# Pairing the value products of successive attention steps and pinning TensorE's order in both mixers of a two-layer encoder trunk

## Chip, cores and metric

The kernel runs on one core of one Trainium2 chip, as one launch. The metric is device time in microseconds, the median of several runs of the same program. TensorE is named PE in the profile, VectorE DVE, ScalarE ACT, GpSimd POOL, and SP is the queue that issues the DMAs.

## The reference

The trunk has two layers on a sequence of 1024 tokens with 1024 features, all in float32, and a final RMSNorm. Layer 0 mixes with two head groups side by side, layer 1 with a chunked band; each mixer is followed by a SwiGLU of width 2816.

```python
# layer 0: MLA (8 heads) | stick-breaking (8 heads), one input projection, one output projection
s_a = (q_a @ k_a.T) * scale_a                       # q_a, k_a from normed latents, with rotary parts
p_a = softmax(where(chunk_ok, s_a, -inf)); o_a = p_a @ v_a
z = (q_b @ k_b.T) * scale_b
log_keep = where(before, log_sigmoid(-z), 0)
w_b = where(before, exp(log_sigmoid(z) + (reverse_cumsum(log_keep) - log_keep)), 0); o_b = w_b @ v_b
h = h + concat(o_a, o_b) @ w_out
# layer 1: every chunk of 64 sees itself and the 8 chunks before it, 16 heads, bias by clipped distance
p = softmax(where(valid, q @ k.T * scale + bias, -inf)); o = p @ v
h = h + o @ w_out
# after each mixer
h = h + (silu(u @ w_gate) * (u @ w_up)) @ w_down    # u = rms_norm(h, g)
```

## The kernel before

Activations stand transposed, features over the 128 partitions, tokens in two halves of 512 columns. A float32 product is done in three matmuls of a shorter float format: each operand is split into a high and a low part (`split`, `weight`, L244 to L269), and `mm3` (L271) multiplies high by high, high by low and low by high. The FFNs use a scheme of seven block products; their order is written out by hand and pinned on all four compute engines.

In the mixers, heads go in pairs: four pairs of stick-breaking, four of MLA, eight of the band. A pair's attention runs over rows (a half of 512 queries) and, in a row, over steps (a block of 128 keys): 4 steps for the first half, 8 for the second. Steps whose block lies on the diagonal work on 512, 384, 256 or 128 columns. A step has stages: in stick-breaking `scores` (L879), `weights` (L897) and `outputs` (L920); in MLA and in the band `front` (scores, exponential, running sum of exponentials) and `back`, which are in `soft_step` (L1044). The last stage is the value product `weighted` (L815): for each of the two heads one matmul of 64 output columns, which the chip does in two passes. So a step shows as four 64-column matmuls on L819 in the profile. After the last step of an MLA or band row, `soft_finish` (L1072) sums the exponentials with ones (64-column matmuls on L1076) and divides.

`step` (L752) keeps a list of steps that still have stages to come. Each call first runs the next stage of every pending step, oldest first, then the first stage of the new step; empty stages set the delay. With `LAG = 2` the delays before the change are: stick-breaking, weights two calls after scores and outputs two calls after weights; MLA, `back` four calls after `front`; band, two calls.

`weave` (L773) interleaves an attention generator with a fill generator (the projections and values of the next pair, or an output projection): after each step it draws fill until the fill's cost is in proportion to the attention done. `with_max` (L1197) draws, after each step from number `skip` on, one group of row maxima (`mla_max`, `band_max`) for a row to come; groups left over when the row ends follow at once. A maximum's end is `neg_max_rows` (L1014): a reduction on VectorE (L1018), transposes of 4 output columns on TensorE (L1021), and VectorE writes (L1023) into the query operand that the scores of that row read. In the band the maxima of a group are passes of VectorE over scores in PSUM (L1166).

PSUM has three kinds of buffers, two of each: `mm` for projections, `o` for value products and norm sums, and `z`, of two banks, for scores, maxima, transposes and denominators. Weights are loaded by the SP queue into four raw buffers and split into four high and four low buffers.

`rstd` (L303) makes a norm's factor: a matmul with ones (L307), then a chain of ScalarE and VectorE operations. `columns` (L333) turns the factor into columns with eight one-column matmuls (L337). `close` (L327) calls both.

Outside the FFNs the order of instructions on each engine is not the source's: a scheduler sorts them by priority and by when it reckons their inputs to be ready. `keep_in_program_order` ties an instruction behind the one traced before it on its engine, as an order of issue alone; `Pinned` wraps an engine so that all its instructions get this.

Of the kernel before, what the change touches and what calls it, by code (L numbers as in the profile page):

```python
# [19 lines left out]
KD = D // P  # L20
# [10 lines left out]
LAG = 2  # L31
# [45 lines left out]
class PinnedCore:  # L77
    def __init__(self, tc):
        nc = tc.nc
        self.sync = nc.sync  # L80
        self.tensor, self.vector, self.scalar, self.gpsimd = (
            Pinned(tc, e) for e in (nc.tensor, nc.vector, nc.scalar, nc.gpsimd))
# [68 lines left out]
class Trunk:  # L151
# [711 lines left out]
    def sb_step(self, p, hf, j, proj, vt, st, o_d):  # L863
        nc = self.nc
# [5 lines left out]
        top = j == 4 * hf + 3  # L870
        c0 = r * P if diag else 0
        cs = slice(c0, HALF)
# [57 lines left out]
        idle = [lambda: None] * (LAG - 1)  # L930
        self.step(scores, *idle, weights, *idle, outputs)
# [112 lines left out]
    def soft_step(self, lag, scores, cs, st, vt, j, first, last, dest):  # L1044
# [25 lines left out]
        self.step(front, *[lambda: None] * (lag - 1), back)  # L1070
# [19 lines left out]
    def mla_attend(self, p, hf, proj, vt, o_d):  # L1090
# [5 lines left out]
        for j in range(nj):  # L1096
# [16 lines left out]
            self.soft_step(2 * LAG, scores, cs, st, vt, j, j == 0, j == nj - 1, (o_d[hf], p, p == 3))  # L1113
# [59 lines left out]
    def band_attend(self, p, hf, proj, tk, vt, o_d):  # L1173
# [5 lines left out]
        for n, j in enumerate(order):  # L1179
# [14 lines left out]
            self.soft_step(LAG, scores, cs, st, vt, j, n == 0, n == len(order) - 1, (o_d[hf], p, p == 7))  # L1194
# [26 lines left out]
    def mixer0(self, h_d):  # L1221
# [5 lines left out]
        with self.phase("mix0", MIX0_TEMPS):  # L1227
# [21 lines left out]
            for p in range(4):  # L1249
                nxt = ([[], []], [[], []], [])  # L1250
                if p < 2:
                    vw = [a["w_vb"][2], a["w_vb"][3]]
                    fill, cost = self.chain(self.sb_project(p + 1, u, nxt), vgen(vw, 1, [p])), 31.0
                elif p == 2:
                    fill, cost = self.chain(self.sb_project(3, u, nxt), self.rope_key(u)), 31.0
                else:
                    fill, cost = prepare(), 73.0
                self.weave(self.ending(self.sb_attend(p, proj, vts[p], o_d)) if p == 3 else
                           self.sb_attend(p, proj, vts[p], o_d), 9.24, fill, cost)
                proj = nxt  # L1260
            for p in range(4):
                nxt = ([[], []], [[], []])
                first, second = (self.mla_attend(p, hf, mla, va[p], o_d) for hf in range(2))
                top = lambda hf: self.mla_max(hf, mla)
                if p < 3:
                    att = self.chain(self.with_max(first, top(1), 0), self.with_max(second, self.mla_max(0, nxt), 4))
                    fill, cost = self.mla_project(p + 1, cq, ckv, nxt), 13.0
                    if p == 2:
                        fill, cost = self.mla_project(3, cq, ckv, nxt, "c", [0]), 8.0
                    self.weave(att, 7.0, fill, cost)  # L1270
                else:
                    o_p = [[None] * KD, [None] * KD]
                    first = self.with_max(first, self.out_loads(o_d[0], 3, o_p[0]), 0)
                    second = self.with_max(second, self.out_loads(o_d[1], 3, o_p[1]), 0)
                    fill = self.chain(self.mla_project(3, cq, ckv, mla, "c", [1]), self.free(top(1)))
                    self.weave(self.ending(first), 2.5, fill, 4.0)
                    o_p[0][3] = o_d[0][3]
                    self.weave(self.ending(second), 6.5, half(0), 41.5)
                    o_p[1][3] = o_d[1][3]
                mla = nxt  # L1280
        return out, half(1, 1)

    def mixer1(self, u, h_d, h2_d):
        a = self.a
        o_d = self.spill("o1_")
        out = Stream()
        half = lambda hf, *e: self.out_half(hf, a["w_out1"], o_p[hf], lambda hf, m: h_d[hf][m], list(range(KD)), out,
                                            h2_d, *e)
        with self.phase("band", BAND_TEMPS):
            vts = [[] for _ in range(8)]  # L1290
            vgen = lambda g, hf: self.values([a["w_v1"][2 * g], a["w_v1"][2 * g + 1]], u, 4, KD, 1,
                                             vts[2 * g:2 * g + 2], hf)
            self.now(vgen(0, [0, 1]))
            new = lambda: ([[], []], [[], []])
            proj = new()
            self.now(self.band_project(0, u, proj))
            tq, tk = self.band_bias(0, "bias_q"), self.band_bias(0, "bias_k")
            self.now(self.band_max(0, proj, tq))
            for p in range(8):
                nxt, fill, cost, tqn, tkn = new(), iter(()), 0.0, None, None  # L1300
                if p < 6:
                    fill = self.chain(self.band_project(p + 1, u, nxt), vgen(p // 2 + 1, [p % 2]))
                    cost = 28.0
                elif p == 6:
                    fill, cost = self.band_project(7, u, nxt, [0]), 16.0

                def late(p=p, nxt=nxt):
                    nonlocal tqn, tkn
                    tqn, tkn = self.band_bias(p + 1, "bias_q"), self.band_bias(p + 1, "bias_k")
                    yield from self.band_max(0, nxt, tqn)  # L1310

                first, second = (self.band_attend(p, hf, proj, tk, vts[p], o_d) for hf in range(2))
                top = self.band_max(1, proj, tq)
                if p < 7:
                    self.weave(self.chain(self.with_max(first, top, 1), self.with_max(second, late(), 4)), 6.8,
                               fill, cost)
                else:
                    o_p = [[None] * KD, [None] * KD]
                    first = self.with_max(first, self.out_loads(o_d[0], 7, o_p[0]), 0)
                    second = self.with_max(second, self.out_loads(o_d[1], 7, o_p[1]), 0)  # L1320
                    fill = self.chain(self.band_project(7, u, proj, [1]), self.free(top))
                    self.weave(self.ending(first), 2.5, fill, 8.0)
                    o_p[0][7] = o_d[0][7]
                    self.weave(self.ending(second), 5.0, half(0), 41.5)
                    o_p[1][7] = o_d[1][7]
                proj, tq, tk = nxt, tqn, tkn
        return out, half(1, 1)

    def run(self):
# [6 lines left out]
        def to_mixer1(hf, m):  # L1336
# [3 lines left out]
            if m == KD - 1:  # L1340
                self.close(nxt, hf, columns=True)
# [135 lines left out]
```

## Time and profile before

| | us |
|---|---|
| three runs | 2614.07, 2611.87, 2613.88 |
| median | 2613.88 |
| the profiled execution, its own time | 2617.44 |
| span of its trace, first to last instruction | 2615.4 |
| mean granted TensorE clock | 0.988 |

In the span the stages lie so: the start of layer 0 up to about 85 us, stick-breaking to 428, MLA to about 600, its output projection and FFN 0 to 1300, the band mixer to about 1900, FFN 1 to the end. An execution's own time is some 2 us above the span. A row of the timeline has the start, the duration, engine, line, operation, tile written and tiles read, shapes (contraction rows * output columns, then partitions x columns) and the count of neighbours merged into it; in square brackets stands the engine's idle time before it and what ended that. A row by groups has busy time and the mean of one in ns behind the bar. A row by windows has the stretch, its length, the busy time of each engine in the order PE, PEld (weight load), DVE, ACT, POOL (engines with nothing are left out), the granted clock and the DMA share.

### The profile page before, as it was taken

Reading aid. Unit: us, or ns where it says so; the run is one execution under the profiler, and the core shown is the slowest. Engines: PE = TensorE matmul, PEld = TensorE weight load, DVE = VectorE, ACT = ScalarE, POOL = GpSimd, SP = SyncE. Lnnn points to the kernel's source line nnn. Section 1 sums busy time; section 2 is a strip of 40 time slices with the busy share of each in tenths; the row PEclk is TensorE's granted clock in tenths of the full one; section 3 lists DMA queues with packets and bytes.
Section 4 is the critical chain, followed back from the end, with each engine's and each line's share of the span. In section 5 each row is a group of like instructions: output and inputs, shape, how many; then the busy total and the mean of one; then the engine's idle time right before and its main releaser. Section 6 shows DMA issues by size and latency. Waiting matters only on the chain.

```text
span 2615.4 us, 33607 instructions
## 1 busy us (share of the span) xinstructions
PE 2523.4 (96%) x11758; PEld 1945.9 (74%) x11758; DVE 1911.0 (73%) x3072; ACT 1169.3 (45%) x2028; POOL 520.4 (20%) x489
## 2 busy tenths in 40 slices
PE   7999999999989999999999999999999999999997
PEld 6766765557878888887887766676777888888776
DVE  6888887775886666677666777777688666667775
ACT  4776676454444434433253333334444443443224
POOL 3333324663000000000022333335300000000004
PEclk9999999999999999999999999999999999999999
DMA  4221100125434334476642222222543434447561
GB/s 137 61 63 53 53 17 29 35 69 160 150 121 141 112 134 145 150 261 215 206 152 67 73 82 80 70 69 89 173 161 119 142 109 137 142 151 258 204 213 69
DMA packets 178856, 318.65 MB, mean 122 GB/s; under 512 B 20480, under 2 KB 36736, under 8 KB 178688
## 3 DMA queue, kind: packets, MB, share of 16 engines
q1 hardware_dynamic: 178688, 316.51, 36.7%
q8 instruction: 93, 1.52, 0.2%
q14 instruction: 75, 0.61, 0.1%
HBM read 221.53 MB, written 84.41 MB: 117 GB/s over the span
## 4 chain that ended last, share of the span: by engine, by line
PE 70%; DVE 12%; issue 2%; ACT 1%; DMA 1%; SPq 0%; DVEq 0%; ACTq 0%
PE z L74 24%; PE mm L74 14%; PE o L74 6%; PE mm L274 5%; PE mm L275 5%; PE mm L276 5%; PE o L819 3%; DVE u L74 2%; DVE f L1081 2%; PE z L1189 1%; PE z L1163 1%; PE z L1190 1%; DVE u L297 1%; PE z L1076 1%; PE z L1108 1%
## 5 line engine op out<-in xcount | busy, mean ns | idle before, releaser
L74 PE MATMUL z<-u,wh 128*128 128x512 f32 x992 | 312.6, 396 | 20.9 <-DVE u L74 13.0
L74 PE MATMUL z<-u,vh 128*128 128x512 f32 x992 | 308.0, 392 | 0.0
L274 PE MATMUL mm<-u,wh 128*128 128x512 f32 x720 | 291.6, 405 | 2.5 <-DVE u L699 1.2
L275 PE MATMUL mm<-u,wh 128*128 128x512 f32 x720 | 284.6, 395 | 1.4 <-DVE u L242 1.4
L276 PE MATMUL mm<-u,wl 128*128 128x512 f32 x720 | 283.8, 394 | 0.0
L242 POOL TENSOR_TENSOR wl<-wr,wh 128x512 fp32r<-128x512 f32 (+2 forms) x95 | 122.7, 1298 | 803.9 <-ACT wh L237 735.3
L74 PEld LDWEIGHTS z<-u,wh 128*128 128x128 f32 x992 | 188.4, 191 | 65.2 <-ACT wh L74 18.0
L74 PE MATMUL mm<-u,wh 128*128 128x512 f32 x720 | 222.5, 390 | 0.0
L74 PEld LDWEIGHTS z<-u,vh 128*128 128x128 f32 x992 | 187.6, 189 | 40.3 <-issue 1.0
L74 PE MATMUL z<-u,wl 128*128 128x512 f32 x496 | 195.5, 394 | 0.0
L74 PE MATMUL z<-u,vl 128*128 128x512 f32 x496 | 193.4, 390 | 0.0
L274 PEld LDWEIGHTS mm<-u,wh 128*128 128x128 f32 x720 | 135.6, 188 | 62.5 <-issue 33.3
L819 PE MATMUL o<-a,u 128*64 128x512 f32 (+3 forms) x768 | 172.3, 485 | 0.3 <-ACT a L1192 0.3
L275 PEld LDWEIGHTS mm<-u,wh 128*128 128x128 f32 x720 | 135.8, 189 | 32.6 <-issue 8.3
L276 PEld LDWEIGHTS mm<-u,wl 128*128 128x128 f32 x720 | 135.6, 188 | 32.2 <-issue 3.7
L74 PEld LDWEIGHTS mm<-u,wh 128*128 128x128 f32 x720 | 135.2, 188 | 28.9 <-issue 1.0
L74 PE MATMUL mm<-u,vh 128*128 128x512 f32 x496 | 152.7, 389 | 0.0
L242 POOL TENSOR_TENSOR u<-wr,u 128x512 fp32r<-128x512 f32 x8 | 10.9, 1373 | 673.6 <-ACT u L237 673.6
L74 PE MATMUL mm<-u,wl 128*128 128x512 f32 x360 | 140.1, 389 | 0.0
L1192 ACT ACTIVATE a<-a 128x1024 f32<-128x1024 f32 (+3 forms) x96 | 70.6, 738 | 155.4 <-DVE a L1191 155.1
L1060 POOL TENSOR_TENSOR b<-b,a 128x512 f32<-128x512 f32 (+3 forms) x80 | 110.5, 1381 | 135.9 <-ACT a L1192 120.4
L1191 DVE TENSOR_TENSOR a<-z,bias 128x1024 f32<-128x1024 f32 (+3 forms) x96 | 78.7, 823 | 79.5 <-PE z L1190 65.5
(246 smaller groups left out, 5972.3 us busy)
## 6 DMA issues: line engine op xcount, KB each, us to landing
u<-f_t SPq DMA_DIRECT2D x144, 256.0 KB, 5.2
vr<-in_w_up SPq DMA_DIRECT2D x88, 256.0 KB, 4.0
wr<-in_w_gate SPq DMA_DIRECT2D x88, 256.0 KB, 3.5
f_t<-x SPq DMA_DIRECT2D x72, 256.0 KB, 2.0
wr<-in_w_out SPq DMA_DIRECT2D x64, 256.0 KB, 3.0
f_t<-e SPq DMA_DIRECT2D x54, 256.0 KB, 3.5
ld<-f SPq DMA_DIRECT2D x54, 256.0 KB, 5.2
h<-u SPq DMA_DIRECT2D x48, 256.0 KB, 2.3
```

The costliest lines, as they stand in the source:

```text
L74: return lambda *a, **k: self.tc.keep_in_program_order(f(*a, **k))
L242: self.eng(eng).tensor_tensor(lo, src, hi.bitcast(F32), ALU.subtract)
L274: mm(out, wh, xh, start=first, stop=False, skip_group_check=onto)
L275: mm(out, wh, xl, start=False, stop=False, skip_group_check=onto)
L276: mm(out, wl, xh, start=False, stop=last, skip_group_check=onto)
L297: self.eng(eng).tensor_tensor(acc, acc, sq, ALU.add)
L819: self.nc.tensor.matmul(o[rh, cs], vt[j // 4][:, j % 4, rh], w[:, e, cs], start=first, stop=last)
L1060: self.eng("dve" if dest[2] else "pool").tensor_tensor(st["esum"][:, :, cs], old[:, :, cs], ex[:, :, cs], ALU.add)
L1076: nc.tensor.matmul(den[64 * e:64 * e + 64, :], self.ones[:, 0:64], esum[:, e, :], start=True, stop=True)
L1081: nc.vector.scalar_tensor_tensor(r, t, 2.0, r, ALU.add, ALU.mult)
L1191: nc.vector.tensor_tensor(ex[:, :, cs], z[:, :, cs], tk[:, :, xs], ALU.add)
L1192: nc.scalar.activation(ex[:, :, cs], ex[:, :, cs], AF.Exp)
```

## The change

`PinnedCore` takes the names of the engines to pin. The pairs' loops of both mixers now run with TensorE alone pinned; the other engines, and the SP queue, stay with the scheduler. The delays are set by the parity of the step, so that a step and its successor have their last stage in the same call: in stick-breaking the outputs come two calls after the weights for odd key blocks and one call after for even ones; in MLA `back` comes four calls after `front` for even steps and three for odd ones; in the band three and two. In the latent norms of MLA, `columns` becomes a piece of its own, drawn later. At the start of the band mixer, the values of the first pairs are formed half by half (each call loads and splits the weights), and the second half's `close`, before made at the end of FFN 0, stands between the first half's values and the first projection.

```diff
-    def __init__(self, tc):
...
+    def __init__(self, tc, names):
+        for n in ("sync", "tensor", "vector", "scalar", "gpsimd"):
+            e = getattr(tc.nc, n)
+            setattr(self, n, Pinned(tc, e) if n in names else e)
...
-    def pinned(self):
-        nc, self.nc = self.nc, PinnedCore(self.tc)
+    def pinned(self, names=("tensor", "vector", "scalar", "gpsimd")):
+        nc, self.nc = self.nc, PinnedCore(self.tc, names)
...
         idle = [lambda: None] * (LAG - 1)
-        self.step(scores, *idle, weights, *idle, outputs)
+        self.step(scores, *idle, weights, *idle[(j + 1) % 2:], outputs)
...
-            self.close(s, hf, (384, 256)[g], g == 1)
+            self.close(s, hf, (384, 256)[g])
             yield
+            if g:
+                self.columns(s, hf, self.out_bank())
+                yield
...
-    def soft_step(self, lag, scores, cs, st, vt, j, first, last, dest):
+    def soft_step(self, n, lag, scores, cs, st, vt, j, first, last, dest):
...
-        self.step(front, *[lambda: None] * (lag - 1), back)
+        self.step(front, *[lambda: None] * (lag - 1 - n % 2), back)
...
-            self.soft_step(2 * LAG, scores, cs, st, vt, j, j == 0, j == nj - 1, (o_d[hf], p, p == 3))
+            self.soft_step(j, 2 * LAG, scores, cs, st, vt, j, j == 0, j == nj - 1, (o_d[hf], p, p == 3))
...
-            self.soft_step(LAG, scores, cs, st, vt, j, n == 0, n == len(order) - 1, (o_d[hf], p, p == 7))
+            self.soft_step(n, LAG + 1, scores, cs, st, vt, j, n == 0, n == len(order) - 1, (o_d[hf], p, p == 7))
...
# mixer0: the loops over the pairs of stick-breaking and of MLA, unchanged, go under
+            with self.pinned(["tensor"]):
...
# mixer1: all of the mixer but its last output half goes under
+            with self.pinned(["tensor"]):
...
-            self.now(vgen(0, [0, 1]))
+                self.now(vgen(0, [0]))
+                self.close(u, 1, columns=True)
...
+                self.now(self.band_project(0, u, proj))
+                self.now(vgen(0, [1]))
...
# run, at the end of FFN 0
-            if m == KD - 1:
+            if m == KD - 1 and hf == 0:
                 self.close(nxt, hf, columns=True)
```

More of the change, by code (lines that the diff above doesn't have):

```diff
@@ L77 @@
 class PinnedCore:
-    def __init__(self, tc):
[L79 to L82, printed above, removed]
+    def __init__(self, tc, names):
+        for n in ("sync", "tensor", "vector", "scalar", "gpsimd"):
+            e = getattr(tc.nc, n)
+            setattr(self, n, Pinned(tc, e) if n in names else e)
 class Pair:
@@ L1247, in prepare @@
                 yield from self.free(self.mla_max(0, mla))
[L1249 to L1280, printed above, removed]
@@ L1289, in mixer1 @@
         with self.phase("band", BAND_TEMPS):
-            vts = [[] for _ in range(8)]
-            vgen = lambda g, hf: self.values([a["w_v1"][2 * g], a["w_v1"][2 * g + 1]], u, 4, KD, 1,
-                                             vts[2 * g:2 * g + 2], hf)
-            self.now(vgen(0, [0, 1]))
[L1294 to L1326, printed above, removed]
@@ new lines, in mixer1, with late @@
+            with self.pinned(["tensor"]):
+                vts = [[] for _ in range(8)]
+                vgen = lambda g, hf: self.values([a["w_v1"][2 * g], a["w_v1"][2 * g + 1]], u, 4, KD, 1,
+                                                 vts[2 * g:2 * g + 2], hf)
+                self.now(vgen(0, [0]))
+                self.close(u, 1, columns=True)
+                new = lambda: ([[], []], [[], []])
+                proj = new()
+                self.now(self.band_project(0, u, proj))
+                self.now(vgen(0, [1]))
+                tq, tk = self.band_bias(0, "bias_q"), self.band_bias(0, "bias_k")
+                self.now(self.band_max(0, proj, tq))
+                for p in range(8):
+                    nxt, fill, cost, tqn, tkn = new(), iter(()), 0.0, None, None
+                    if p < 6:
+                        fill = self.chain(self.band_project(p + 1, u, nxt), vgen(p // 2 + 1, [p % 2]))
+                        cost = 28.0
+                    elif p == 6:
+                        fill, cost = self.band_project(7, u, nxt, [0]), 16.0
+                    def late(p=p, nxt=nxt):
+                        nonlocal tqn, tkn
+                        tqn, tkn = self.band_bias(p + 1, "bias_q"), self.band_bias(p + 1, "bias_k")
+                        yield from self.band_max(0, nxt, tqn)
+                    first, second = (self.band_attend(p, hf, proj, tk, vts[p], o_d) for hf in range(2))
+                    top = self.band_max(1, proj, tq)
+                    if p < 7:
+                        self.weave(self.chain(self.with_max(first, top, 1), self.with_max(second, late(), 4)), 6.8,
+                                   fill, cost)
+                    else:
+                        o_p = [[None] * KD, [None] * KD]
+                        first = self.with_max(first, self.out_loads(o_d[0], 7, o_p[0]), 0)
+                        second = self.with_max(second, self.out_loads(o_d[1], 7, o_p[1]), 0)
+                        fill = self.chain(self.band_project(7, u, proj, [1]), self.free(top))
+                        self.weave(self.ending(first), 2.5, fill, 8.0)
+                        o_p[0][7] = o_d[0][7]
+                        self.weave(self.ending(second), 5.0, half(0), 41.5)
+                        o_p[1][7] = o_d[1][7]
+                    proj, tq, tk = nxt, tqn, tkn
```

32 lines of the change are left out of this document (added).

## The prediction

> **What bounds the kernel now.** I read the page first, then the busy times by stretch, then the order of instructions on TensorE.
>
> ```profile
> span 2615.4 us, 33607 instructions
> PE 2523.4 (96%) x11758; PEld 1945.9 (74%) x11758; DVE 1911.0 (73%) x3072; ACT 1169.3 (45%) x2028; POOL 520.4 (20%) x489
> PE 70%; DVE 12%; issue 2%; ACT 1%; DMA 1%; SPq 0%; DVEq 0%; ACTq 0%
> ```
>
> The chain that ended last runs over TensorE for 70% and over VectorE for 12%. Busy TensorE time is no measure of full speed, since ends are modelled and neighbours overlap. So I go by starts. The next rows are busy times by stretch; the column behind POOL is the granted clock, and (x...) counts instructions.
>
> ```profile
> 100.00:200.00 100.00, 97.25 (x506) 70.94 (x505) 89.56 (x110) 73.27 (x106) 39.73 (x50) 1.00 0.22 60
> 1532.00:1594.30 62.30, 60.40 (x330) 43.20 (x328) 45.63 (x92) 23.09 (x41) 22.38 (x22) 1.00 0.26 77
> 2000.00:2100.00 100.00, 100.00 (x443) 82.81 (x442) 66.24 (x106) 42.09 (x77) 0.00 (x0) 1.00 0.43 147
> 1470.33:1490.55 20.22, 19.06 (x94) 13.21 (x92) 18.12 (x48) 6.74 (x11) 3.98 (x3) 1.00 0.21 58
> 424.50:428.40 3.90, 0.76 (x5) 0.28 (x4) 3.77 (x7) 1.50 (x4) 2.12 (x2) 0.97 0.17 45
> 428.40:432.40 4.00, 3.95 (x9) 3.14 (x10) 3.03 (x5) 1.56 (x2) 1.26 (x1) 0.50 0.02 5
> ```
>
> In the FFN (2000 to 2100) 443 matmuls of 512 columns fill 100 us, 0.226 us each, with nothing lost; the change doesn't touch that. One head pair of the band mixer takes 62.3 us (1532 to 1594.3; seven follow one another at this pace). In stick-breaking (100 to 200) VectorE is busy 89.6 us of 100, and in a part of each band pair (1470.33 to 1490.55) 18.12 us of 20.22. In these two places TensorE isn't alone in setting the time.
>
> **The gain, term by term: fewer changes of tile width.** A value product is four 64-column matmuls (two heads, two passes each) among 128-column ones:
>
> ```profile
> 303.26 0.39 PE L276 MATMUL mm<-u,wl 128*128 128x512 f32 x1
> 303.57 1.08 PE L819 MATMUL o<-a,u 128*64 128x512 f32 x4
> 304.58 0.50 PE L904 MATMUL z<-c,masks 128*128 128x256 f32 x2
> 304.92 0.40 PE L907 MATMUL z<-b,masks 128*128 128x256 f32 x2
> 305.15 0.39 PE L909 MATMUL z<-c,masks 128*128 128x256 f32 x2
> 506.92 1.03 PE L1076 MATMUL z<-b,ones 128*64 128x512 f32 x4
> 507.88 0.50 PE L1108 MATMUL z<-u,u 100*128 100x512 f32 x1
> ```
>
> Going in: 303.26 to 303.57 is 0.31 us where 0.23 is the pace, 0.08 lost. Going out: the product holds TensorE 1.01 us, while the same shape that starts inside a run of 64 columns (the denominator at 506.92, behind a value product) takes 0.96, 0.05 lost. Then the first pair of wide matmuls takes 304.92 - 304.58 = 0.34 us and the next 0.23, 0.11 lost. One run costs about 0.25 us.
>
> ```profile
> L819 PE MATMUL o<-a,u x768: 272/486/1116, 85.8 to 1895.9; 128*64 128x512 f32 x72, 128*64 128x128 f32 x40, 128*64 128x256 f32 x40, 128*64 128x384 f32 x40
> ```
>
> 768 / 4 = 192 steps. Counted in the timeline between these two times they stand, with the denominators, in 213 runs of 64 columns: 52 in stick-breaking, 50 in MLA, 111 in the band. With pairs, 96 runs remain (24, 24, 48), since a row has 4 or 8 steps, the delays of neighbours meet in one call of the step function, and a denominator follows its last product. 117 x 0.25 = **-29 us**.
>
> ```profile
> 490.30 1.07 PE L819 MATMUL o<-a,u 128*64 128x512 f32 x2
> 491.30 1.20 PE L1037 MATMUL z<-u,u 96*128 96x512 f32 x4
> 492.44 1.07 PE L819 MATMUL o<-a,u 128*64 128x512 f32 x2
> 493.44 0.50 PE L274 MATMUL mm<-u,wh 128*128 128x512 f32 x1
> ```
>
> Here the free order tore the two heads of one step apart: each half takes 1.00 us, as long as the whole at 303.57, because the heads no longer run side by side. I count 45 such half runs (14 of 512 columns, 8 of 384, 11 of 256, 12 of 128), at one pass of 0.48 us for 512 and in proportion below. Pinned order can't do it: **-14 us**. Gain in all -43 us.
>
> **The cost: what the free order hid.** Pinned, the first matmul that waits holds up all behind it. I walk through the band in source order. In a pair, row maxima for the second half are formed after steps 1, 2 and 3 of the first half; the fourth group, the transposes (L1021) and the first scores of the second half then come back to back, without fill. Now:
>
> ```profile
> 1475.49 1.08 PE L819 MATMUL o<-a,u 128*64 128x512 f32 x4
> 1477.72 0.39 PE L1189 MATMUL z<-u,u 128*128 128x256 f32 x1 [1.16 <-DVE m L1166]
> 1489.70 0.39 PE L275 MATMUL mm<-u,wh 128*128 128x512 f32 x1
> 1490.02 0.60 PE L1021 MATMUL z<-ident,m 128*4 128x128 f32 x4
> 1490.55 0.50 PE L1189 MATMUL z<-u,u 128*128 128x512 f32 x1
> 1470.33:1490.55 20.22, 12.69 (x47) 8.37 (x47) 1.37 (x2) 0.00 (x0) 1.00 0.21 58
> ```
>
> The last row is the same stretch for the fill's bank `mm` alone: 47 fill matmuls lie between the second scores and the transposes' readers. By source, steps 1 to 3 draw 28/6.8 x (0.75+0.5+0.25) = 6.2 of cost, ten items of 0.648, about 29 matmuls. So 18 x 0.227 = 4.1 us of fill leaves the stretch. VectorE's work there stays, and the transposes need its end:
>
> ```profile
> 1470.33:1490.55 20.22, 8.29 (x32) 1.00 0.21 58
> L1166 DVE CUSTOM_DVE_ANT_0 z<-z,bias 128x512 f32<-128x512 f32 x4 | 2.8, 698 | 0.0
> L1081 DVE SCALAR_TENSOR_TENSOR f<-f,f 128x512 f32<-128x512 f32 x1 | 2.3, 2307 | 0.0
> 1471.41 0.96 DVE L1191 TENSOR_TENSOR a<-z,bias 128x768 f32<-128x768 f32 x1 [4.11 <-PE z L1190]
> ```
>
> The first row is VectorE's time for the maxima alone (L1166, sixteen passes of 128 to 512 columns). Without the 18 fill matmuls TensorE has 20.2 - 4.1 - 1.2 (the wait shown) - 0.8 (two runs saved, some) = 14.1 us of work. VectorE needs 18.1 us plus 0.9 to its start and about 1.4 through the transposes: a stall of 6.3 us. If two casts for the values (1.4 us) and one eviction (2.1 us) fall elsewhere, for instance into the 4.11 us in which VectorE waits ahead of the stretch, 2.8 us are left. With two banks of scores only, a third group of maxima waits for the addition on the first, which can bring it to 7.8. I take 5 (2.8 to 7.8). At the end of a pair the same happens once more, with one group of 512 (two of 0.70 us) and some fill between: 2 us (1 to 2.5). Against the 1.2 us waited now: +5.8 a pair, seven pairs, **+41 us** (15 to 58).
>
> The last pair has its maxima of the second half in a bunch behind its fill: +5 (0 to 8). The moved `close` of the second half puts ones-matmul and columns one behind the other:
>
> ```profile
> 1357.20 1.07 PE L307 MATMUL o<-u,ones 128*128 128x512 f32 x2
> 1362.03 1.05 PE L337 MATMUL o<-ones,u 1*128 1x1 f32 x8
> ```
>
> That chain lasts 4.8 us, now under fill, then open but for its own 0.5: +4.3. The first maxima (eight passes, half of 8.29, 4.1 us, and 1.4 through the transposes, against 1.3 us of TensorE work) lose the projection that covers them: +4. The second value call loads and splits its weights again (four loads of 256 KB, four casts on ScalarE, four subtractions on VectorE); the projection of 22 us ahead hides these, and without it some 3 us would show. Together **+8** (4 to 12).
>
> ```profile
> L1039 DVE TENSOR_REDUCE m<-z 128x2 f32<-128x1024 f32 x6 | 7.3, 1223 | 4.5 <-PE z L1037 4.5
> 428.40:600.00 171.60, 165.18 (x714) 99.38 (x715) 129.50 (x153) 81.31 (x128) 105.04 (x72) 0.97 0.16 50
> ```
>
> In MLA the maxima are plain reductions (1.22 us for 512 columns of two heads) and a pair's value products stand ahead of the scores that need them; but its fill runs out before the last steps. I reckon 6 us of waits for each of four pairs. The stretch now has 171.6 - 165.2 = 6.4 us idle and at a clock of 0.97 some 5 more: 24 - 11.4, **+12** (0 to 22).
>
> In stick-breaking 28 runs are saved, 7 us, but VectorE stands at 89.6%; the later step of each pair also has its weights only one step ahead. Half of it I give back: **+4** (0 to 12). The latent norms' split-off columns need no new wait; they give the chain of 4.8 us two fill items of cover, and the last of them is open today as well: 0 (-5 to +7). Queues of SP and POOL keep their order free.
>
> Sum: -43 + 41 + 5 + 8 + 12 + 4 = +27 on the profiled 2617.4, thus 2644; the median of the runs shown is 3.6 lower, so **2640 us**.
>
> **Rivals.** *Faster.* VectorE's order stays free: its scheduler can put the finishing (L1080 to L1082) and evictions behind the maxima. Then only the maxima (8.3) and three additions (0.96 us and, by width, 0.64 and 0.32) stand before the transposes, within TensorE's 14.1 us, and the stall falls to about 1 us. The band then costs 7 x 1.8 = 13, MLA 4, the last pair 0: -43 + 13 + 4 + 8 + 4 = -14, near 2600, with lower ends everywhere 2575. For it speaks the 4.11 us idle row, against it that L1081 of 2.3 us stands amid the maxima today. With my other costs it decides at a stall of 1.3 us in that place.
>
> *The clock falls too.* After 3.9 us with 0.76 us of matmuls (424.5) the granted clock was 0.50 for 4 us: 2 us lost. If each of eight band pairs and four MLA pairs does this, +24: 2664. For it speaks that row; against it, that my stalls come in pieces of 1 to 2.4 us. [...]
>
> *No change.* Costs end near 43 us by chance.
>
> **How the numbers follow.** Forecast 0.44; clock 0.18; faster 0.28; even 0.10, nearly all within 0.2% (5 us, about what a measurement of this kernel can tell from no change). Faster 0.28, same 0.08, slower 0.64. The range runs from 2588, inside the faster case, to 2685, above the clock case with some costs at their upper ends. The forecast's own range is 2622 to 2660.
>
> **What would show it.** Runs of 64 columns near 96, none with half a step. Band pairs near 66 us, with idle TensorE ahead of L1021 and of the second half's L1189, ended by VectorE (L1018, L1023), and ahead of L1163 ended by L1191. A bare 4 to 5 us between L307 and L337 near 1340. The FFN unchanged. The prediction is wrong if band pairs come out under 62 us: then VectorE's chain was shorter than I walked it. If they exceed 68, look for a clock under 1.00.

## The result, and the profile after

The changed kernel takes **2847.01 us** (median of four runs, 2841.28 to 2849.78); beside it the kernel before took 2613.98 (four runs, 2611.87 to 2614.77). The ratio is 1.0885, with a 95% interval from 1.0871 to 1.0898. Forecast were 2640 us and a range from 2588 to 2685: the sign was right, the size was not. The profiled execution of the changed kernel took 2844.88 us, with a span of 2842.9.

From the page of the changed kernel, its span and the busy times of the engines:

```profile
span 2842.9 us, 33626 instructions
PE 2567.9 (90%) x11758; PEld 1998.4 (70%) x11758; DVE 1941.6 (68%) x3076; ACT 1177.8 (41%) x2032; POOL 517.3 (18%) x489
```

TensorE was busy for 2523.4 of 2615.4 us and is busy for 2567.9 of 2842.9: 183 us more are idle, and it is busy 44 us longer with the same 11758 matmuls.

Next, busy times by stage. I cut the stages at matmuls that every kernel here has: stick-breaking (with the preparation of MLA) from the first sum with the masks to MLA's first maximum, MLA up to its last matmul of 104 rows, the start of mixer 1, and the band from its first to its last matmul of 68 rows. Idle time of TensorE is the length less the first busy time. The kernel before:

```profile
78.10:417.80 339.70, 326.00 (x1519) 231.15 (x1518) 292.18 (x365) 240.33 (x365) 119.50 (x142) 0.98 0.17 48
417.80:647.50 229.70, 219.18 (x952) 138.46 (x951) 162.56 (x194) 107.19 (x168) 126.94 (x89) 0.98 0.24 75
1303.80:1408.50 104.70, 101.66 (x540) 85.58 (x539) 61.90 (x104) 43.41 (x80) 26.23 (x28) 1.00 0.40 127
1408.50:1892.90 484.40, 471.67 (x2471) 332.27 (x2470) 358.97 (x725) 189.18 (x329) 186.23 (x173) 1.00 0.29 89
```

The changed kernel, the same four stages and then one pair of the band:

```profile
76.70:486.90 410.20, 337.68 (x1529) 246.64 (x1530) 304.15 (x367) 246.05 (x369) 118.13 (x145) 0.90 0.14 40
486.90:785.70 298.80, 237.32 (x948) 153.78 (x947) 179.16 (x192) 105.47 (x165) 124.33 (x87) 0.83 0.18 57
1444.30:1555.00 110.70, 100.13 (x517) 84.05 (x516) 65.50 (x108) 45.92 (x84) 26.09 (x28) 0.94 0.41 130
1555.00:2123.60 568.60, 492.29 (x2495) 360.15 (x2494) 359.23 (x725) 192.25 (x329) 187.89 (x173) 0.92 0.24 76
1646.40:1717.10 70.70, 61.93 (x331) 45.85 (x329) 44.97 (x94) 23.41 (x42) 22.68 (x23) 0.93 0.21 67
```

Stick-breaking grew by 70 us, MLA by 69, the band by 84, the start of mixer 1 by 6; FFN 0 took 2 us more, FFN 1 3 us less. In stick-breaking TensorE's idle time went from 13.7 to 72.5 us, in MLA from 10.5 to 61.5, in the band from 12.7 to 76.3. In all three the granted clock fell, in MLA from 0.98 to 0.83.

Where the band waits, by groups of matmuls (behind the second bar the idle time before them and what ended it; nearly all matmuls of the pinned region are recorded on L74, the wrapper's line, so the tiles tell them apart; L1020 is L1018 of before, L1168 is L1166, L1193 is L1191). The kernel before:

```profile
L1189 PE MATMUL z<-u,u 128*128 128x128 f32 (+3 forms) x191 | 65.9, 356 | 5.7 <-DVE m L1166 5.7
L1021 PE MATMUL z<-ident,m 128*4 128x128 f32 x60 | 9.0, 273 | 0.2 <-DVE m L1018 0.2
```

The changed kernel, in which scores and maxima are one group:

```profile
L74 PE MATMUL z<-u,u 128*128 128x128 f32 (+5 forms) x472 | 134.2, 369 | 41.3 <-DVE a L1193 16.9 <-DVE m L1168 15.9 <-DVE u L241 5.8
L74 PE MATMUL z<-ident,m 128*4 128x128 f32 x60 | 11.9, 334 | 32.0 <-DVE m L1020 32.0
```

These are places that the prediction walked: the transposes behind VectorE's reduction (32.0 us; 0.2 before), and scores and maxima that wait for a bank of scores, which either a maximum's pass (15.9) or an addition (16.9) has to free. One of these places in time order, with some rows left out:

```profile
1718.48 0.73 PE L74 MATMUL z<-u,u 128*128 128x512 f32 x2 [1.14 <-DVE m L1168]
1722.37 0.60 PE L74 MATMUL z<-ident,m 128*4 128x128 f32 x4 [3.16 <-DVE m L1020]
1724.12 1.06 PE L74 MATMUL z<-u,u 128*128 128x512 f32 x2
1724.97 1.06 PE L74 MATMUL mm<-u,wh 128*128 128x512 f32 x2
```

Two waits of 1.14 and 3.16 us, and then the matmuls start 0.43 us apart (two from 1724.12 to 1724.97) where 0.23 is the pace. The same stretch in four parts of 3.41 us, cut where the recorded clock falls (1723.06) and rises (1726.48):

```profile
1716.24:1719.65 3.41, 1.83 (x9) 1.12 (x7) 3.41 (x13) 1.86 (x4) 0.74 (x1) 1.00 0.01 2
1719.65:1723.06 3.41, 0.69 (x5) 0.43 (x5) 2.87 (x8) 0.00 (x0) 0.00 (x0) 1.00 0.45 93
1723.06:1726.48 3.42, 3.42 (x8) 2.42 (x9) 2.23 (x3) 0.00 (x0) 0.00 (x0) 0.50 0.72 255
1726.48:1729.89 3.41, 3.41 (x16) 2.77 (x16) 0.00 (x0) 1.06 (x1) 0.40 (x2) 1.00 0.01 2
```

A part with 2.72 us idle (3.41 less 0.69) is followed by a part at half clock: 8 matmuls instead of 16. In the part behind it the pace is back.

Mixer 0, which the prediction had not walked through, by groups in stick-breaking:

```profile
L74 PE MATMUL z<-c,masks 128*128 128x512 f32 (+3 forms) x192 | 56.8, 385 | 17.3 <-DVE a L914 15.0 <-DVE c L241 1.4 <-ACT c L891 0.6
L74 PE MATMUL o<-a,u 128*64 128x512 f32 (+3 forms) x192 | 44.2, 576 | 8.0 <-ACT a L915 4.1 <-POOL a L875 3.8
L74 PE MATMUL mm<-wl,u 128*128 128x256 f32 (+1 forms) x80 | 26.6, 332 | 18.8 <-DVE wl L241 18.8
L74 PE MATMUL o<-u,ones 128*128 128x512 f32 x8 | 6.3, 876 | 14.9 <-DVE u L296 14.9
L74 PE MATMUL o<-ones,u 1*128 1x1 f32 x16 | 2.9, 299 | 3.8 <-DVE u L313 3.8
```

and in MLA:

```profile
L74 PE MATMUL z<-u,u 100*128 100x512 f32 (+8 forms) x381 | 102.3, 409 | 40.2 <-DVE m L1041 20.6 <-ACT a L1113 13.6 <-ACT u L236 3.2
L74 PE MATMUL z<-ident,m 128*4 128x128 f32 x32 | 7.3, 372 | 12.0 <-DVE m L1020 12.0
```

Among them are single waits longer than any that I had assumed. The first row is a matmul that forms values and whose low weight part comes late; the second waits for the sum of squares of a latent norm, and the third for a bank that a maximum of MLA still reads:

```profile
129.53 0.58 PE L74 MATMUL mm<-wl,u 128*128 128x256 f32 x1 [9.41 <-DVE wl L241]
444.45 2.04 PE L74 MATMUL o<-u,ones 128*128 128x512 f32 x2 [10.59 <-DVE u L296]
551.61 2.68 PE L74 MATMUL z<-u,u 104*128 104x384 f32 x8 [3.98 <-DVE m L1041]
```

### The profile page after: what moved, and what is told of

It reads as the page before. It is cut to its first block, busy times and chain, and to the rows that moved or that the text cites. A ratio compares the mean times of both kernels' runs of the same rounds, so it can differ in the third digit from the quotient of the medians.

```text
span 2842.9 us, 33626 instructions
## 1 busy us (share of the span) xinstructions
PE 2567.9 (90%) x11758; PEld 1998.4 (70%) x11758; DVE 1941.6 (68%) x3076; ACT 1177.8 (41%) x2032; POOL 517.3 (18%) x489
## 4 chain that ended last, share of the span: by engine, by line
PE 66%; DVE 14%; ACT 2%; issue 2%; DMA 1%; DVEq 0%; SPq 0%; ACTq 0%
PE z L74 29%; PE mm L74 26%; PE o L74 9%; DVE u L74 2%; DVE z L1168 2%; DVE f L1083 1%; DVE m L1041 1%; DVE u L995 1%; PE mm L275 1%; PE mm L273 1%; PE mm L274 1%; DVE u L296 1%; DMA ld<-f 1%; DVE a L1193 1%; DVE u L241 1%
## 5 line engine op out<-in xcount | busy, mean ns | idle before, releaser
L74 PE MATMUL mm<-u,wh 128*128 128x512 f32 x2000 | 641.2, 403 | 4.3 <-DVE f L979 3.2
L74 PEld LDWEIGHTS mm<-u,wh 128*128 128x128 f32 x2000 | 385.1, 195 | 89.9 <-issue 10.3
L74 PE MATMUL mm<-u,wl 128*128 128x512 f32 x1000 | 398.9, 399 | 0.0
L74 PE MATMUL z<-u,u 128*128 128x128 f32 (+15 forms) x1056 | 284.0, 382 | 85.0 <-DVE m L1041 20.6
L74 PE MATMUL z<-u,wh 128*128 128x512 f32 x992 | 311.5, 394 | 22.7 <-DVE u L74 14.8
L74 PEld LDWEIGHTS z<-u,u 128*128 128x128 f32 (+4 forms) x1056 | 190.4, 209 | 184.9 <-issue 49.8
L74 PE MATMUL z<-u,vh 128*128 128x512 f32 x992 | 307.2, 391 | 0.0
L74 PEld LDWEIGHTS z<-u,wh 128*128 128x128 f32 x992 | 187.7, 190 | 67.0 <-ACT wh L74 18.5
L74 PEld LDWEIGHTS mm<-u,wl 128*128 128x128 f32 x1000 | 193.8, 194 | 42.7
L74 PEld LDWEIGHTS z<-u,vh 128*128 128x128 f32 x992 | 187.3, 189 | 40.1 <-issue 1.0
L74 PE MATMUL z<-u,wl 128*128 128x512 f32 x496 | 195.2, 394 | 0.0
L74 PE MATMUL z<-u,vl 128*128 128x512 f32 x496 | 193.3, 390 | 0.0
L1193 DVE TENSOR_TENSOR a<-z,bias 128x1024 f32<-128x1024 f32 (+3 forms) x96 | 78.9, 823 | 157.2 <-PE z L74 146.7
L74 PE MATMUL o<-a,u 128*64 128x512 f32 (+3 forms) x768 | 153.5, 522 | 11.5 <-ACT a L915 4.1
L74 PE MATMUL mm<-u,vh 128*128 128x512 f32 x496 | 152.7, 389 | 0.0
L74 PE MATMUL mm<-wh,u 128*128 128x256 f32 (+1 forms) x672 | 136.7, 294 | 3.0 <-ACT u L812 3.0
L74 DVE TENSOR_TENSOR wl<-wr,wh 128x512 fp32r<-128x512 f32 (+1 forms) x190 | 122.9, 652 | 5.5 <-ACT wh L74 5.5
L74 ACT CAST wh<-wr 128x512 fp32r<-128x512 f32 (+1 forms) x190 | 109.6, 583 | 39.0 <-DVE wr L74 31.7
```

The costliest lines, as they stand in the source:

```text
L74: return lambda *a, **k: self.tc.keep_in_program_order(f(*a, **k))
L1193: nc.vector.tensor_tensor(ex[:, :, cs], z[:, :, cs], tk[:, :, xs], ALU.add)
```

## Experiments

**Theories.** Theory 1: the pinned order costs, as fill no longer slips into waits, and the pairing gains. Theory 2: the pairing's changed delays make the waits. Fifteen kernels follow; the table has their times and the lengths of three stages, delimited as above. Times without a range in the text are of one execution, and every stage is of one trace.

| kernel | us | stick-breaking | MLA | band |
|---|---|---|---|---|
| before | 2613.98 | 339.7 | 229.7 | 484.4 |
| changed | 2847.01 | 410.2 | 298.8 | 568.6 |
| e1 delays alone, free order | 2625.23 | 345.4 | 240.9 | 480.6 |
| e2 pinned, old delays | 2813.3 | 376.8 | 281.4 | 584.2 |
| e3 VectorE pinned too in mixer 0 | 2974.64 | 561.6 | 270.5 | 569.0 |
| e4 narrow maxima, pinned | 2818.59 | 408.5 | 295.6 | 546.3 |
| e5 tied pairs, free order | 2614.78 | 348.5 | 233.7 | 474.8 |
| e6 idle matmuls, pinned | 2832.65 | 411.4 | 293.4 | 557.3 |
| e7 values' low parts on GpSimd | 2846.41 | 400.9 | 298.8 | 578.8 |
| e8 maxima one step earlier | 2849.74 | 411.5 | 298.8 | 571.9 |
| e9 tied pairs with slack, free | 2614.18 | 344.8 | 236.3 | 475.0 |
| e10 pairs in the band, early singles | 2628.37 | 346.8 | 249.6 | 476.2 |
| e11 changed, with slack | 2808.54 | 382.3 | 288.1 | 572.2 |
| e12 narrow maxima, before | 2611.44 | 339.9 | 229.4 | 481.6 |
| e13 changed, fill in the waits | 2785.96 | 408.9 | 288.4 | 525.4 |
| e14 e13 with slack | 2765.16 | 382.2 | 287.9 | 531.1 |
| e15 pairs in the band alone, free | 2605.07 | 340.5 | 227.4 | 475.6 |

### Which half of the change costs: e1, e2

```diff
# e1: on the kernel before
-        self.step(scores, *idle, weights, *idle, outputs)
+        self.step(scores, *idle, weights, *idle[(j + 1) % 2:], outputs)
# likewise the parity delays of soft_step; no pinning
# e2: on the changed kernel, the old delays back; pinning and moved closes stay
```

> The kernel before with the three delays by parity alone; TensorE's order stays free. Theory 1 (the pinned order costs, the pairing gains): the scheduler still tears many pairs apart, its stream has 161 runs of 64 columns (before 213, after 94) and 35 half steps (before 45), so 52 x 0.25 + 10 x 0.3 = 16 us are gained: about 2598 us, 2585 to 2615. Theory 2 (the changed delays make the waits, by tiles held longer and weights only one step ahead): most of the 233 us stay, over 2750 us.

> The changed kernel with the old delays: TensorE pinned, moved closes kept, no pairs. Theory 1: the waits stay and 183 runs of 64 columns instead of 94 cost 89 x 0.25 = 22 us more: about 2869 us, clock at or under 0.945. Theory 2 (delays): back near 2614 us plus the 6 us of the moved close.

e1: 2625.23 us (2621.31 to 2628.28), ratio 1.0042 (1.0028 to 1.0056): a small loss instead of a gain of 16. The free order tears pairs apart more than I had counted: its trace has 62 runs that hold half a step, the kernel before 48 (45 by the prediction's count). The band gains 3.8 us, stick-breaking and MLA lose 5.7 and 11.2; what makes these losses e1 alone doesn't show. e2: 2813.3 us, 34 below the changed kernel, where Theory 1 had 22 above. The stages by busy times (stick-breaking, MLA, band):

```profile
77.00:453.80 376.80, 331.15 (x1530) 236.98 (x1531) 297.85 (x367) 245.86 (x369) 115.79 (x145) 0.95 0.15 43
453.80:735.20 281.40, 234.83 (x949) 149.51 (x947) 170.28 (x192) 106.18 (x165) 125.45 (x87) 0.85 0.19 61
1504.20:2088.40 584.20, 506.87 (x2494) 358.26 (x2494) 358.08 (x725) 192.37 (x329) 188.60 (x173) 0.91 0.23 74
```

The pinned order, with the moved closes, costs 37, 52 and 100 us: Theory 1 holds for most of the loss. On top of it the pairs cost 33 us in stick-breaking and 17 in MLA, and bring 16 in the band. So Theory 2 holds in mixer 0, where the later step of a pair lost a call of slack, and not in the band, where the earlier one won a call.

### Is the gain there at all: e5, e9, e10, e15

```diff
# e5, on the kernel before; order free; back/outputs of a pair meet in one call
+        with self.tc.high_priority(offset=400):
+            for i, (j, w, cs, first, last) in enumerate(prods):   # the later step first
...
+                    m = self.nc.tensor.matmul(o[rh, cs], vt[j // 4][:, j % 4, rh], w[:, e, cs], start=first, stop=last)
+                    if i or e:
+                        self.tc.keep_in_program_order(m)
# e9: e5, and in mixer 0 one call more of delay, "a": (5, 1024), HEAP = 59
# e10: e5's pairs in the band; in mixer 0 old delays, single products tied and early
# e15: e5's pairs in the band; mixer 0 as before
```

> The kernel before, TensorE's order free, but the two value products of a pair issued as one group: the product of the later step first, the other three matmuls tied behind it in order, the group with a higher priority in the scheduler; nothing else is pinned. Its stream has 125 runs of 64 columns (before 213) and no half step (before 45). Theory 1 (the gain of the pairing is real, the cost is the pinned order alone): 88 x 0.25 + 14 = 36 us less, about 2578 us (2565 to 2600), clock still near 0.99. Theory 2 (pairing by itself makes waits): no better than 2614.

> As the tied pairs in free order (2614.8 us, where some 40 us of width changes and half steps were saved and some 42 us of new waits came in stick-breaking, MLA and band), with one call more between weights and outputs in stick-breaking (three and two) and between front and back in MLA (five and four), one more step buffer, and for its room one heap tile less. Theory 2a (the pair's later step had lost a call of slack, and this makes the waits): the waits of stick-breaking and MLA go back by 20 to 30 us, about 2590. Rival (stick-breaking is held by VectorE at 90%, and waits of TensorE there only take the place of the saved time): within 8 us of 2614.

> TensorE's order free; pairs tied as before, but in the band alone; in stick-breaking and MLA single value products with the old delays, the two heads tied and early, so that no half step is left. From the stages of the tied pairs: the band gains 9.6 us, stick-breaking and MLA lose their 8.8 and 3.9 and gain some of the 12 us that half steps cost them: about 2597, 2588 to 2606. If the gain in the band too is only given back elsewhere: 2614.

> The kernel before, TensorE's order free, with tied pairs in the band alone; stick-breaking and MLA untouched, their old delays and no early products. Theory (the early, tied products are what disturbed MLA in the run with pairs in the band, 229.8 to 249.7 us, and stick-breaking, 339.7 to 346.8): these two stages stay within 2 us of before and the band's 8 to 10 us remain: about 2605, 2602 to 2608. Rival (the free order of one stage shifts with anything changed, and gains are drowned): 2610 or more.

e5: 2614.78 us, ratio 0.9999 (0.9988 to 1.0010): nothing gained with 88 runs fewer. Its three stages:

```profile
78.50:427.00 348.50, 319.08 (x1521) 237.37 (x1520) 298.27 (x365) 240.85 (x366) 120.55 (x144) 0.97 0.16 47
427.00:660.70 233.70, 216.01 (x958) 140.09 (x957) 154.60 (x193) 106.79 (x167) 125.96 (x86) 0.93 0.22 72
1419.10:1893.90 474.80, 459.12 (x2472) 332.63 (x2470) 342.65 (x725) 190.12 (x329) 190.40 (x173) 1.00 0.28 90
```

Against before TensorE is busy 22.6 us less in the three and idle 25.8 us more. The gain exists and is turned into waits, 15.7 us of them in stick-breaking, where VectorE stands at 298 of 348 us. One call of slack (e9: 2614.18, ratio 1.0001, 0.9991 to 1.0010) brings back 3.7 of the 8.8 us lost in stick-breaking and loses 2.6 in MLA: in free order lost slack is at most a small part of the cause. e10 (2628.37, ratio 1.0057, 1.0040 to 1.0074) missed its 2597: with the old delays and only early, tied single products MLA got 20 us longer. So what disturbs MLA there comes with these products, tied and early; whether the tie or the higher priority does it, and by which wait, stays open. e15 leaves mixer 0 alone: **2605.07 us** (2601.53 to 2611.63), ratio 0.9968 (0.9956 to 0.9979), faster than both kernels. Its stages, and the band's value products before (first fence) and in e15 (last):

```profile
L819 PE MATMUL o<-a,u 128*64 128x384 f32 (+3 forms) x376 | 76.2, 460 | 0.3 <-ACT a L1192 0.3
```

```profile
74.00:414.50 340.50, 326.84 (x1519) 231.44 (x1519) 292.72 (x365) 240.44 (x365) 120.79 (x142) 0.98 0.16 48
414.50:641.90 227.40, 216.62 (x953) 136.62 (x951) 163.07 (x194) 107.15 (x168) 126.91 (x89) 0.99 0.24 76
1402.10:1877.70 475.60, 461.20 (x2471) 334.71 (x2470) 340.58 (x725) 190.15 (x329) 190.11 (x173) 0.99 0.28 90
```

```profile
L821 PE MATMUL o<-a,u 128*64 128x512 f32 (+3 forms) x376 | 64.0, 456 | 1.5 <-ACT a L1213 1.1
```

The 376 recorded value products take 64.0 us instead of 76.2. About half of this is that no head runs alone any more: in the trace of the kernel before, the 18 half runs took 9.7 us, and at the rate of its whole steps their columns would have taken 3.9. The rest goes with the longer runs. The band keeps 8.8 us, TensorE's busy time falls by 10.5.

### What the pinned band waits for: e4, e12, e8, e13

```diff
# e4 on the changed kernel, e12 on the kernel before: narrow maxima (the other columns are left out)
-                    nc.vector.tensor_tensor_reduce(out=z[:, e, :n], in0=z[:, e, :n], in1=tq[:, e, y0:y0 + n],
+                    nc.vector.tensor_tensor_reduce(out=z[:, e, :P], in0=z[:, e, :P], in1=tq[:, e, y0:y0 + P],
# e8: maxima one step earlier
-                    self.weave(self.chain(self.with_max(first, top, 1), ...
+                    self.weave(self.chain(self.with_max(first, top, 0), ...
# e13: fill behind left-over groups of maxima (totals of weave 8.0 and 7.6)
         for _ in maxes:
-            pass
+            yield 0.6 if skip < 4 else 0.0
```

> The changed kernel with VectorE's passes for the band's row maxima cut to 128 columns each (0.28 us instead of 0.28 to 0.73; the maxima over the other columns are left out, TensorE's work is the same). A pair has 24 such passes, 5.4 us less on VectorE, 3.6 of them in the first half's chain. Theory 1 (VectorE's chain of maxima holds the transposes and what is queued behind them): the waits of some 4 us at the end of the first half and of 1.3 at the second's shrink to under 1, the clock stays at 1.00 and a band pair falls from 70.5 to about 62; the band from 569 to about 500, the whole about 2780. Rival (the waits come from the order itself, over the banks of scores): under 15 us of change.

> The kernel before with VectorE's passes for the band's row maxima cut to 128 columns (the maxima over the other columns are left out); the same cut took 22 us off the pinned band. Theory (in free order fill hides this chain): at most the six waits for it go, 6.2 us; the band 478 to 485, the whole 2607 to 2615. Rival (VectorE's chain holds the band in both orders): the band falls by about 20.

> The changed kernel with the first half's groups of row maxima of the band drawn from step 0 on instead of step 1, so that the last group has fill behind it before the transposes and the second half's scores. Theory 1: the waits at the end of each pair's first half (about 4.4 us) fall to 1 to 2, the clock there stays up, a band pair falls from 70.5 to 65 or 66, the whole about 2810. Rival (the maxima start before VectorE has the bias and the query rows, and the wait moves to the front of the pair): under 10 us of change.

> The changed kernel with fill drawn also behind the left-over groups of row maxima: twelve matmuls of a projection between the fourth group and the transposes, nine to twelve between the transposes and the first scores of the second half (in MLA only the second of these). No instruction is added or taken away. Theory 1 (the waits of the pinned order come from where the source puts the fill, and the free order had moved it there): in the band the waits at the transposes fall from 32 us to under 15, the whole idle time from 76 to about 45, the clock rises from 0.92 to 0.97 or more, and the band comes from 569 to 520 to 535; MLA from 299 to about 290; the whole about 2800. Rival (the drawn fill is missed elsewhere and the waits move there): under 15 us of change.

e4: the band falls by 22 us, not by 69. By groups:

```profile
L74 PE MATMUL z<-u,u 128*128 128x128 f32 (+5 forms) x472 | 132.3, 366 | 33.2 <-DVE a L1193 20.7 <-DVE u L241 5.0 <-DVE m L1168 4.3
L74 PE MATMUL z<-ident,m 128*4 128x128 f32 x60 | 9.8, 289 | 17.0 <-DVE m L1020 17.0
```

Waits for the passes themselves (L1168) went from 15.9 to 4.3 and the transposes' from 32.0 to 17.0, while the waits behind the additions (L1193) grew from 16.9 to 20.7. VectorE's chain of maxima is a part, the additions in the same queue are another. The same narrow passes in the kernel before (e12: 2611.44) take 2.8 us off the band: in the free order the chain is nearly hidden. e8: less idle time (the transposes' waits fall to 25.1), but no gain:

```profile
1555.90:2127.80 571.90, 505.53 (x2494) 369.65 (x2494) 358.82 (x725) 192.33 (x329) 188.65 (x173) 0.91 0.24 75
```

Idle time is 66.4 us instead of 76.3, and busy time 505.5 instead of 492.3 at a clock of 0.91. Shorter waits alone did not help. The lower clock accounts for some 8 of the 13 us of busy time (an estimate: 571.9 x (1 - 0.910) less 568.6 x (1 - 0.924)); the rest isn't explained. e13 draws fill into both waits, with no instruction added:

```profile
1539.20:2064.60 525.40, 473.98 (x2494) 351.05 (x2494) 351.75 (x725) 192.00 (x329) 187.15 (x173) 0.97 0.25 82
```

```profile
L74 PE MATMUL z<-ident,m 128*4 128x128 f32 x60 | 10.6, 308 | 17.6 <-DVE m L1020 17.6
```

The band falls by 43 us, half of the change's loss there: 25 us less idle and, with the clock up from 0.92 to 0.97, 18 us less busy. So the place where the source puts its fill makes a good part of these waits, and each us of idle time removed brought 1.7 us. The transposes still wait 17.6 us, where under 15 were expected.

### Mixer 0: e3, e7, e11, e14

```diff
# e3, mixer 0 alone
-            with self.pinned(["tensor"]):
+            with self.pinned(["tensor", "vector"]):
# e7
-        ws = [self.weight(x, eng_lo="dve") for x in wsrc]
+        ws = [self.weight(x, eng_lo="pool") for x in wsrc]
# e11: changed kernel, "a": (5, 1024), HEAP = 59, one call more of delay in mixer 0; e14: e11 and e13 together
```

> The changed kernel with VectorE pinned to the source's order beside TensorE in mixer 0 (not in the band). Theory 1a (mixer 0 waits because VectorE's free order puts work that the next matmul needs behind work that nobody needs yet, as the 9.4 us for the low part of a value weight): stick-breaking with the preparation falls from 410 to about 350 us and MLA from 299 to about 260; the whole about 2745. Theory 1b (a strict TensorE order waits whatever order VectorE has, since the chains from scores to weights are longer than the source puts work between them): mixer 0 stays within 20 us of 709, the whole 2830 to 2870, and with two strict orders perhaps more.

> The changed kernel with the low parts of the value weights formed on GpSimd instead of VectorE. Theory 1a: the two waits of 9.5 us for that subtraction at about 120 and 209 us, and the lower clock behind them, go: stick-breaking from 410 to about 385 us, the whole about 2822. Rival: another late operation takes their place, under 8 us of change.

> The changed kernel with the same additional call of slack in stick-breaking and MLA. Theory 2a: its share of the waits that the pairs add under a pinned order (33 us in stick-breaking, 17 in MLA over the kernel with the order pinned and old delays) goes: about 2800. Theory 1b (the pinned order waits at norms, maxima, exponentials and scores, which slack for the products doesn't touch): within 15 us of 2847.

> The same with the additional call of slack and the step buffer of the run on slack in mixer 0. If the two causes lie side by side, the gains add: stick-breaking 382, MLA about 280, the band as with the fill alone, the whole 38 us under the run with the fill alone, about 2760. If they share waits, less than 25 us under it.

e3: 2974.64 us, and stick-breaking takes 561.6:

```profile
81.30:642.90 561.60, 364.69 (x1531) 266.53 (x1531) 291.00 (x370) 249.66 (x368) 120.68 (x143) 0.81 0.10 30
```

```profile
L74 PE MATMUL mm<-u,wh 128*128 128x512 f32 x406 | 141.6, 433 | 44.8 <-DVE wh L74 37.5 <-DVE u L74 7.0 <-ACT u L812 0.3
L74 PE MATMUL mm<-u,wl 128*128 128x512 f32 x204 | 88.2, 432 | 43.4 <-DVE wl L74 43.4
L74 PE MATMUL mm<-wl,u 128*128 128x256 f32 (+1 forms) x80 | 27.7, 346 | 28.6 <-DVE wl L74 28.4
```

TensorE is idle for 197 us of it, 109 of them ahead of projections whose weight parts VectorE now forms late. Its free order was a help, and Theory 1a falls in stick-breaking; MLA got 28 us shorter, which is the way that Theory 1a had it there. e7: the 18.8 us of waits for low parts go and stick-breaking is only 9 us shorter, as value products now wait 11.9 us for GpSimd instead of 3.8; the band, whose values changed too, is 10 us longer. GpSimd is busy 221.82 us there instead of 187.89, but TensorE's idle time hardly grew (78.0 us against 76.3); its busy time rose by 8.5, at a clock of 0.911 instead of 0.924. In sum nothing. e11: stick-breaking falls to 382.3 and MLA to 288.1, the whole to 2808.54, as Theory 2a had it. By groups:

```profile
L74 PE MATMUL o<-a,u 128*64 128x512 f32 (+3 forms) x192 | 37.6, 514 | 1.1 <-ACT a L915 1.1
L74 PE MATMUL mm<-wl,u 128*128 128x256 f32 (+1 forms) x80 | 26.1, 326 | 0.0
L74 PE MATMUL o<-u,ones 128*128 128x512 f32 x8 | 6.4, 889 | 15.2 <-DVE u L296 15.2
```

With one call more the products hardly wait (1.1 us instead of 8.0), and the waits for `wl` vanish though nothing of that weight was changed: so in the pinned kernel they too hung on the lost slack. The norm's 15.2 us stay; e2 has them too (15.5). e14: 2765.16 us, 21 below e13 where 38 was expected; stick-breaking adds up exactly (382.2), MLA (287.9) shares its gain with the fill, and the band is 6 us longer than in e13.

### The clock: e6

```diff
         mt = self.banks()
+        for _ in range(8):
+            nc.tensor.matmul(mt[:, 0, :], self.zeros, self.masks, start=True, stop=True)
```

> The changed kernel with eight idle matmuls of 512 columns (1.8 us) on TensorE ahead of the transposes of each group of maxima, in the band and in MLA; their product is overwritten. Theory 1 (the waits are filled, not shortened, and it is the lowered clock behind them that costs the other half): band clock from 0.92 to 0.98 or more, band from 569 to 530 to 550, MLA a little lower; the whole about 2800. Rival (the clock falls with the waits' number or is no cost, or the idle matmuls only stand in the way): 24 groups x 1.8 = 43 us more, about 2890.

2832.65 us, 14 below the changed kernel. The band:

```profile
1554.50:2111.80 557.30, 505.70 (x2613) 368.83 (x2614) 358.97 (x725) 192.12 (x329) 187.91 (x173) 0.97 0.24 77
```

```profile
L74 PE MATMUL z<-masks 128*128 128x512 f32 x120 | 32.8, 418 | 2.3 <-DVE m L1170 2.2
```

120 recorded idle matmuls (27 us at 0.227) made the band 11 us shorter. Idle time fell by 25 us; busy time rose by 13, so the useful matmuls were busy 14 us less, at a clock of 0.97 instead of 0.92. The rival's 43 us more did not come. Theory 1 had the band at 530 to 550 and the whole at about 2800: its direction held, its size did not, and 51.6 us of idle time stayed in the band, 42.0 of them ahead of scores and maxima.

## Why the prediction failed, by its steps

**Runs of 64 columns, -29, and half steps, -14: right in count, right in size where it can be seen.** The changed kernel has 94 runs and no half step (96 and none predicted). In e15's band, 43 runs and 18 half runs went. Counted from the starts of the matmuls there, the changes of width cost 20.9 us instead of 30.6, 0.23 us for each run that went (0.25 predicted), and the half steps 6 us less. Of these 16 us the band kept 8.8; 1.7 us went into more idle time and some 3.4 into two parts of 3.41 us at half clock (about 1440 to 1446.6, where fill matmuls of 256 columns start 0.21 us apart instead of 0.12), and the last 2 I can't place. What failed is that I carried this gain to the end of the kernel as time. In free order e5 had it on TensorE and lost as much; under the pinned order the pairs gained in the band alone.

**Stalls of the band, +41 (15 to 58), and +5 for the last pair: mechanism and place right, idle time forecast too low, time wrong.** A pair's idle time rose from 1.9 us (the prediction's row from 1532) to 8.8, that is by 6.9 where 5.8 stood. The wait ahead of the transposes was 3.16 and the one ahead of it 1.14, against 5 walked. Over the stage idle time grew by 63.6 us against 46. The range was added up wrongly too: a pair's pieces (2.8 to 7.8 and 1 to 2.5, less 1.2) give 18 to 64 for seven pairs. A pair lasts 70.7 us, not 66; 1.1 us of this is idle time beyond the forecast, and most of the rest goes with its clock of 0.93.

**The clock: the step that was mis-weighed everywhere.** I had it as a rival of 0.18 and +24 us, because "my stalls come in pieces of 1 to 2.4 us". Length less clock-weighted length is 2842.9 x (1 - 0.945) = 156 us against 31 before. TensorE's busy time grew by 44 us although the changes of width and the half steps saved it some 40 (119 runs at 0.23 us and 48 half runs at about 0.3), so the low clock cost some 80 us (an estimate from these two numbers) of the 227 by which the span grew; 183 are idle time.

**MLA, +12 (0 to 22), and stick-breaking, +4 (0 to 12): the steps that failed most.** With the pairing's share of -29 and -14 these stages should have gained a little; they lost 69 and 70 us. I had walked neither in source order, only reckoned "6 us of waits for each of four pairs" and "Half of it I give back". MLA's idle time came to 61.5 us where 24 were reckoned, at a clock of 0.83 where none was taken off. The runs show the pinned order, with the moved closes, at 52 us in MLA and 37 in stick-breaking (e2). Its waits there are, in MLA, transposes behind the reduction (14.0 us), maxima's banks (13.4) and scores behind exponentials (9.0), and in stick-breaking the norms' sum of squares (15.5) and sums behind subtractions (9.5); no run takes these away one by one. Then comes the lost slack, which the prediction named ("only one step ahead") and priced inside those 4 us: 28 us in stick-breaking and 11 in MLA (e11).

**Latent norms, 0 (-5 to +7): wrong.** The ones-matmuls wait 14.9 us and the columns 3.8, where 1.3 and 1.4 us stood before:

```profile
L307 PE MATMUL o<-u,ones 128*128 128x512 f32 x8 | 5.2, 739 | 1.3 <-DVE u L297 1.3
```

These 16 us more lie inside the stage that is called stick-breaking above. I had looked at the columns and not at the sum of squares, which VectorE forms last (L296) while TensorE's queue stands still for 10.59 us.

**The start of mixer 1, +8 (4 to 12): right.** 104.7 to 110.7 us; the columns wait 4.06 us for the factor, as the chain of 4.8 less its own time had it:

```profile
1509.74 1.86 PE L74 MATMUL o<-ones,u 1*128 1x1 f32 x8 [4.06 <-DVE u L313]
```

The rival "faster" needed a band stall under 1.3 us in that place; it was 4.3 (1.14 and 3.16).

## What to carry to other kernels

With one engine pinned, here, late operands that the free order had hidden became idle time of its whole queue (183 us more). So walk each stage that is pinned, in source order, not just the one with the clearest chain; the stages that I had only estimated made up 140 of the 227 us by which the span grew. Time saved on an engine was kept only where new waits did not take it (e5, 2614.78 us, against e15, 2605.07): tie just the few instructions that belong together and leave the rest free (e15), and check what slack the tie takes from the step that comes later. If an order must be pinned, draw the fill into the waits: in the band that brought back half of the loss (e13).

## What the runs showed of the hardware

**Behind some of the waits the granted clock was 0.50.** In the trace of the kernel before it was 0.50 for 61 us of the span, in that of the changed kernel for 314; in the band for none and for 86. In the stretch shown above, the wait of 1.14 us and the first 0.44 of the next add up to 1.58 us of idle time in one part, and the part behind it was still at 1.00; the other 2.72 us of that wait were followed by 0.50. Another place of the same trace had less idle time and lost the clock all the same: from 1760.61 to 1764.02 TensorE was idle for 1.13 us, and from 1764.02 to 1767.43 the clock was 0.50. So how much idle time it takes is not shown. The prediction had set its "pieces of 1 to 2.4 us" against a drop; in these places 1.58 us did not bring one and 1.13 us did.

**In e8 less idle time came with no higher clock.** TensorE was idle in its band for 66.4 us instead of the changed kernel's 76.3, and the granted clock was 0.91 instead of 0.92. Why it was no higher is not shown.
